# Two products instead of three for the last 32 gate channels of an RWKV output projection

## The chip, the cores and the metric

The kernel runs on one core of one Trainium2 chip. The metric is the device time of one execution in microseconds (us); the time before is 2402.96 us, the median of 3 runs (2399.5 to 2404.71). The verdict compares runs of the two kernels on the same chip.

## The reference, cut to what matters

A two-layer decoder trunk over 16 learned tokens and 512 tokens of 1024 channels. Layer 0 is an RWKV-7 time mixing between two half-step SwiGLU blocks, layer 1 a sparse attention between two more. Only the gate of the time mixing is touched here:

```python
D_GATE_LORA = 160
g = jax.nn.sigmoid(xg @ g1) @ g2              # g1: 1024 x 160, g2: 160 x 1024
...
return ((yn + bonus) * g) @ w_o               # the output projection, 1024 x 1024
```

## The kernel before, in words

Every product of the heavy matrices is done in three passes for precision. An operand is split into `hi`, its value in the shorter 32-bit type that the profile calls fp32r, and `lo`, what is left of it; `mm3` (L496) adds hi x hi, lo of the data x hi of the weights, and hi of the data x lo of the weights into one PSUM bank. The weights stream from DRAM in an order that is fixed ahead (`Weights`, L178): a unit is 1024 columns, SyncE loads it into `wraw`, ScalarE writes `whi`, VectorE writes `wlo` (L211), two units ahead of the product that takes them. So each unit costs ScalarE and VectorE one long instruction, and those stand in their queues between the others, in program order.

The tokens go through in two ranges, A (272 tokens, padded to 288) and B (256). For each range the time mixing has a projection stage (`proj`, L802; pools pA and pB), a chunked recurrence that is interleaved with other work by a planner (`run`, L729), and an output projection (`outproj`, L1270; pools oA and oB, L1352 and L1359). The planner orders side work by an estimated clock; what it decides after this change is the same order of instructions.

The gate stands in two places. In `proj`, step `g1` (L936 to L948), for each of 8 blocks of 128 input channels, two `mm3` go into two banks: 128 gate channels, then the last 32, with a stationary operand 32 columns wide. A sigmoid writes them to `R.sg`, the last 32 in partitions 0 to 31 of its second half. In `outproj`, `R.sg` is split into `shi` and `slo` (both named `lhi` and `llo` in the profile). Then `gate(m)` (L1279), for each of 8 blocks m of 128 output channels, does six products into a bank `bg`: three on 128 rows and three on 32 rows:

```python
for k, q in ((0, 128), (1, 32)):
    w = W.take(blk("g2", k, m))
    mm3(p[:, :n], (w[0][:q], w[1][:q]), (shi[:q, k, :n], slo[:q, k, :n]), k == 0, k == 1)
```

VectorE takes the bank, adds a bias to the recurrence's output and multiplies (`tb`), ScalarE writes `o_hi`, VectorE `o_lo`. These are the data of `wo`. The order is written by hand: gates 0 to 2; then for d = 0 to 7 the gate d + 3 (while there is one) and nine products of `wo` on `o[d]` into three banks; then the other five output blocks with 24 products each. On VectorE `tb` and `o_lo` of one gate stand one behind the other, so it waits for `o_hi` between them.

Of the kernel before, what the change touches and what calls it, by code (L numbers as in the profile page):

```python
# [10 lines left out]
F32 = mybir.dt.float32  # L11
F32R = mybir.dt.float32r
I32 = mybir.dt.int32
AF = mybir.ActivationFunctionType
OP = mybir.AluOpType
AX = mybir.AxisListType

D = 1024
DT = 8
# [32 lines left out]
def blk(key, k, m):  # L52
    return (key, k, m * 128, (m + 1) * 128)
# [124 lines left out]
class Weights:  # L178
# [32 lines left out]
    def split(self, last):  # L211

        while self.nlo <= min(last, len(self.units) - 1):
            self.round(self.nlo)
            r = self.raw.pop(self.nlo)
            w = r.shape[1]
            lo = self.pool.tile([128, 1024], F32R, name="wlo", bufs=self.bufs)
            self.nc.vector.tensor_sub(lo[:, :w], r, self.hi[self.nlo][:, :w].bitcast(F32))
            self.lo[self.nlo] = lo
            self.nlo += 1  # L220
# [213 lines left out]
def trunk(ctx, tc, wall, units, h0, vec, cstd, gqk, out, stop=None, gap=0.0, share=400.0, slack=200.0, fulls={}):  # L434
    clock = Clock()
    nc = Core(tc.nc, clock)
# [12 lines left out]
    W = Weights(nc, wpool, wall, units, raw_bufs=4, bufs=4, ahead=2)  # L449
# [46 lines left out]
    def mm3(p, w, x, first, last):  # L496

        nc.tensor.matmul(p, w[0], x[0], start=first, stop=False)
        nc.tensor.matmul(p, w[0], x[1], start=False, stop=False)
        nc.tensor.matmul(p, w[1], x[0], start=False, stop=last)  # L500

    def split(hi, lo, src, gp=False):
        nc.scalar.activation(hi, src, AF.Copy)
        if gp:
            nc.gpsimd.tensor_tensor(lo, src, hi.bitcast(F32), op=OP.subtract)
        else:
            nc.vector.tensor_sub(lo, src, hi.bitcast(F32))


    def newton(y, x, it, a):  # L510
# [291 lines left out]
    def proj(R, norm, sp, core, XB):  # L802

        r, n, pad, nch = R.r, R.n, R.pad, R.nch
# [14 lines left out]
        def mix(i, d):  # L819

            x = work.tile([128, 288], F32, name="tb", bufs=4)
            nc.vector.scalar_tensor_tensor(x[:, :n], xx[d // 4][:, d % 4, :n], col(MIX + 8 * i + d),
                                           hn[d][:, 1:1 + n], op0=OP.mult, op1=OP.add)
            hi = sp.tile([128, 288], F32R, name="xm_hi", bufs=XB)
            lo = sp.tile([128, 288], F32R, name="xm_lo", bufs=XB)

            def make():
                split(hi[:, :n], lo[:, :n], x[:, :n], gp=True)
                xm[i, d] = (hi[:, :n], lo[:, :n])

            if late:
                late.pop()()
            late.append(make)
# [70 lines left out]
        ps, pl, pg = {}, None, None  # L904
        for kind, *st in proj_steps():
            if kind == "d":
                key, g, ds = st
                if ds[0] == 0:
                    ps = [bank() for _ in range(4)]
                x = [need(mixof[key], d) for d in ds]  # L910
                mixes(len(ds))
                for m, p in enumerate(ps, 4 * g):
                    for d in ds:
                        w = W.take(blk(key, d, m))
                        yield p[:, :n], *w, *x[d - ds[0]]
                        mm3(p[:, :n], w, x[d - ds[0]], d == 0, d == DT - 1)
                    if ds[-1] == DT - 1:
                        evac(key, m, p[:, :n])
                free[0] += g * len(ds)
                mixes(g * len(ds))  # L920
                yield
            elif kind == "lora":
                key, d = st
                if pl is None:
                    pl = bbank("ry")
                mm3(pl[:, :n], W.take(blk(key, d, 0)), need(mixof[key], d), st == ["lw", 0], st == ["la", DT - 1])
                free[0] += 1
                mixes(1)
                if st == ["la", DT - 1]:
                    lora_end(pl)  # L930
                yield
            elif kind == "wa2":
                decay(st[0])
                yield
            elif kind in "EP":
                powers(kind, st[0])  # L936
            else:
                d = st[0]
                pg = pg or (bank(), bank())
                x = need(5, d)  # L940
                for m, k in ((0, 128), (1, 32)):
                    w = W.take(blk("g1", d, m))
                    mm3(pg[m][:k, :n], (w[0][:, :k], w[1][:, :k]), x, d == 0, d == DT - 1)
                free[0] += 1
                mixes(1)
                if d == DT - 1:
                    for i, k in ((0, 128), (1, 32)):
                        sg = R.sg[:k, i, :n]  # L948
                        nc.scalar.activation(sg, pg[i][:k, :n], AF.Sigmoid)
                yield  # L950
# [319 lines left out]
    def outproj(R, sp, nxt):  # L1270

        n, pad, r = R.n, R.pad, R.r
        shi = sp.tile([128, 2, 288], F32R, name="lhi")
        slo = sp.tile([128, 2, 288], F32R, name="llo")
        for i, k in ((0, 128), (1, 32)):
            split(shi[:k, i, :n], slo[:k, i, :n], R.sg[:k, i, :n])
        xs = {}

        def gate(m):  # L1279
            p = bbank()  # L1280
            for k, q in ((0, 128), (1, 32)):
                w = W.take(blk("g2", k, m))
                mm3(p[:, :n], (w[0][:q], w[1][:q]), (shi[:q, k, :n], slo[:q, k, :n]), k == 0, k == 1)
            t = work.tile([128, 288], F32, name="tb", bufs=4)
            nc.vector.scalar_tensor_tensor(chunks(t[:, :n]), R.AR[:, m, :R.nch, 1], col(LNB + m),
                                           chunks(p[:, :n]), op0=OP.add, op1=OP.mult)
            hi = sp.tile([128, 288], F32R, name="o_hi", bufs=8)
            lo = sp.tile([128, 288], F32R, name="o_lo", bufs=8)
            split(hi[:, :n], lo[:, :n], t[:, :n])
            xs[m] = (hi[:, :n], lo[:, :n])  # L1290

        def end(m, p):
            residual(m, r, p[:, pad:n], 1.0)
            nxt.add(m, r)

        for m in range(3):
            gate(m)
            yield
        ps = [bank() for _ in range(3)]
        for d in range(DT):  # L1300
            if d + 3 < DT:
                gate(d + 3)
            for m in range(3):
                mm3(ps[m][:, :n], W.take(blk("wo", d, m)), xs[d], d == 0, d == DT - 1)
            yield
        for m in range(3):
            end(m, ps[m])
        for m in range(3, DT):
            p = bank()
            for d in range(DT):  # L1310
                mm3(p[:, :n], W.take(blk("wo", d, m)), xs[d], d == 0, d == DT - 1)
                yield
            end(m, p)
# [404 lines left out]
def lay_out(i):  # L1718
    f = {k: np.asarray(v) for k, v in i.items()}

    def cols(a):
        return a.reshape(-1, DT, 128).transpose(2, 0, 1).reshape(128, -1)

    def qk_gain(a):

        return np.tile(np.concatenate([np.ones(16, np.float32), a[0, 16:]]), 2)[:, None]

    def pad(a, rows, width, c0=0):
        z = np.zeros((rows, width), np.float32)
        z[:a.shape[0], c0:c0 + a.shape[1]] = a  # L1730
        return z

    mats = {}
    for l in range(2):
        for j in range(2):
            mats[f"win{l}{j}"] = f["ffn_w_in"][l, j]
            mats[f"wout{l}{j}"] = f["ffn_w_out"][l, j]
    for k in "rkvo":
        mats["w" + k] = f["rk_w_" + k][0]
    mats["lw"] = pad(f["rk_w1"][0], D, 128)  # L1740
    mats["la"] = pad(f["rk_a1"][0], D, 128, 64)
    mats["wa2"] = np.concatenate([f["rk_w2"][0], f["rk_a2"][0]])
    mats["g1"] = pad(f["rk_g1"][0], D, 256)
    mats["g2"] = pad(f["rk_g2"][0], 256, D)
    w = f["at_w_in"][0]
    mats["idx"] = w[:, 1536:2120]
    mats["kvq"] = np.concatenate([w[:, 1024:1536], w[:, :1024]], 1)
    mats["ao"] = f["at_w_o"][0]
    vec = np.concatenate([cols(f["norm_g"]), cols(f["rk_mix"])] +
                         [cols(f["rk_" + k]) for k in ("w0", "a0", "k_k", "k_a", "r_k", "lnx_g", "lnx_b")] +  # L1750
                         [qk_gain(f["at_q_g"]), qk_gain(f["at_k_g"])], 1)
    h0 = np.concatenate([f["meta"], f["x"][0]], 0).T.reshape(DT, 128, T).transpose(1, 0, 2)
    return {"h0": np.ascontiguousarray(h0), "vec": np.ascontiguousarray(vec), "cst": constants(),
            "gqk": np.concatenate([f["at_q_g"], f["at_k_g"]], 0)}, mats
# [17 lines left out]
```

## Time and profile before

| | |
|---|---|
| median of 3 runs | 2402.96 us |
| the profiled execution's own time | 2405.28 us |
| its span, first to last instruction | 2403.5 us |
| TensorE (PE), matrix products | 2335.7 us busy, 97% |
| VectorE (DVE) | 1706.2 us, 71% |
| ScalarE (ACT) | 1263.9 us, 53% |
| GpSimd (POOL) | 169.5 us, 7% |
| mean granted TensorE clock | 0.982 of full speed |

The profile gives each instruction its start and duration. Products overlap in the profile: the time that one costs in a run of them is the distance of two starts, not the duration shown. The granted clock is shown as a share of 2.4 GHz: 1.00 is 2.4 GHz and 0.50 is 1.2 GHz, the two levels there are. The shape of a product is given as rows*columns of its stationary operand, then partitions x columns of the moving one: `32*128 32x256` is a product over 32 rows that gives 128 output channels for 256 tokens.

### The profile page before, as it was taken

To read this page: it belongs to the slowest core of one execution; us is meant where nothing else is said; L and a number is where in the kernel's file an instruction comes from. 1 tells how busy PE (TensorE), PEld (TensorE's weight loads), DVE (VectorE), ACT (ScalarE), POOL (GpSimd) and SP (SyncE) were. 2 spreads that over 40 slices of the span, in tenths; PEclk is the share of its full clock that TensorE was granted. 3 is DMA by queue.
4 is the path that set the end of the run, shared out by engine and by line. 5 is a ranking of instruction groups with operands and counts; after the bars stand their busy time and mean duration, and the time that the engine had idled before them with its cause. 6 is when DMAs were issued, how large, how long until landed. Compare 5 with 4: busy or idle time off the path is not lost.

```text
span 2403.5 us, 49406 instructions
## 1 busy us (share of the span) xinstructions
PE 2335.7 (97%) x20122; PEld 2189.8 (91%) x20122; DVE 1706.2 (71%) x3337; ACT 1263.9 (53%) x2125; POOL 169.5 (7%) x215
## 2 busy tenths in 40 slices
PE   8998999999889999999999999999999999999999
PEld 8997889998789899999999999799888888879999
DVE  7667888856787975576566566687767888666765
ACT  5443664456448535644444444456665546565543
POOL 0001521010043011000000000000000000000000
PEclk9999999999899999999999999999999999999999
DMA  6553335542334454244555555454434444425554
GB/s 228 174 177 114 125 125 172 172 133 72 106 115 159 153 164 133 81 132 153 176 176 167 186 190 177 140 168 142 150 122 138 141 144 133 139 78 168 177 185 141
DMA packets 101491, 356.13 MB, mean 148 GB/s; under 512 B 11520, under 2 KB 15632, under 8 KB 101264
## 3 DMA queue, kind: packets, MB, share of 16 engines
q1 hardware_dynamic: 99120, 347.91, 43.8%
q0 software_dynamic: 2144, 5.07, 0.8%
q8 instruction: 158, 2.59, 0.4%
q14 instruction: 69, 0.57, 0.1%
HBM read 348.60 MB, written 4.33 MB: 147 GB/s over the span
## 4 chain that ended last, share of the span: by engine, by line
PE 53%; DVE 2%; ACT 1%; issue 0%; DVEq 0%; ACTq 0%
PE acc L341 46%; PE bg L341 6%; PE ry L341 1%; DVE wlo L341 1%; DVE qst L341 0%; ACT whi L341 0%; DVE h L341 0%; DVE pr L341 0%; DVE tb L341 0%; DVE xa_lo L341 0%; DVE m L341 0%; DVE rel L341 0%; DVE nst L341 0%; DVE hid_lo L341 0%; ACT xa_hi L341 0%
## 5 line engine op out<-in xcount | busy, mean ns | idle before, releaser
L341 ACT ACTIVATE whi<-wraw 128x1024 fp32r<-128x1024 f32 (+1 forms) x658 | 688.5, 1051 | 465.2 <-PE acc L341 274.8
L341 DVE TENSOR_TENSOR wlo<-wraw,whi 128x1024 fp32r<-128x1024 f32 (+1 forms) x658 | 809.8, 1234 | 170.8 <-ACT whi L341 170.1
L341 PE MATMUL acc<-hid_hi,whi 128*128 128x256 f32 (+1 forms) x1408 | 412.1, 293 | 6.0 <-DVE h L341 5.9
L341 PE MATMUL acc<-hid_lo,whi 128*128 128x256 f32 (+1 forms) x1408 | 399.5, 284 | 0.0
L341 PE MATMUL acc<-hid_hi,wlo 128*128 128x256 f32 (+1 forms) x1408 | 399.4, 284 | 0.0
L341 PE MATMUL acc<-xa_hi,whi 128*128 128x256 f32 (+1 forms) x1088 | 316.4, 291 | 1.8 <-ACT xa_hi L341 1.4
L341 PE MATMUL acc<-x_hi,whi 128*128 128x272 f32 (+1 forms) x1024 | 303.1, 296 | 8.7 <-ACT whi L341 6.2
L341 PE MATMUL acc<-xa_hi,wlo 128*128 128x256 f32 (+1 forms) x1088 | 309.0, 284 | 0.1
L341 PE MATMUL acc<-xa_lo,whi 128*128 128x256 f32 (+1 forms) x1088 | 308.9, 284 | 0.1
L341 PE MATMUL acc<-x_hi,wlo 128*128 128x272 f32 (+1 forms) x1024 | 294.9, 288 | 0.5 <-DVE wlo L341 0.5
L341 PE MATMUL acc<-x_lo,whi 128*128 128x272 f32 (+1 forms) x1024 | 294.5, 288 | 0.1
L341 PEld LDWEIGHTS acc<-hid_hi,whi 128*128 128x128 f32 x1408 | 265.5, 189 | 23.0 <-issue 12.2
L341 PEld LDWEIGHTS acc<-hid_lo,whi 128*128 128x128 f32 x1408 | 266.9, 190 | 0.2 <-DVE hid_lo L341 0.2
L341 PEld LDWEIGHTS acc<-hid_hi,wlo 128*128 128x128 f32 x1408 | 265.8, 189 | 0.0
L341 PEld LDWEIGHTS acc<-xa_hi,whi 128*128 128x128 f32 x1088 | 206.2, 190 | 19.7 <-issue 17.1
L341 PE MATMUL acc<-xb_hi,whi 128*128 128x256 f32 x752 | 215.4, 286 | 0.0
L341 PE MATMUL acc<-xb_lo,whi 128*128 128x256 f32 x752 | 210.7, 280 | 0.0
L341 PE MATMUL acc<-xb_hi,wlo 128*128 128x256 f32 x752 | 210.6, 280 | 0.0
L341 PEld LDWEIGHTS acc<-x_hi,whi 128*128 128x128 f32 x1024 | 194.9, 190 | 15.2 <-ACT whi L341 6.2
L341 PEld LDWEIGHTS acc<-xa_lo,whi 128*128 128x128 f32 x1088 | 206.6, 190 | 0.6 <-DVE xa_lo L341 0.5
L341 PEld LDWEIGHTS acc<-xa_hi,wlo 128*128 128x128 f32 x1088 | 206.2, 190 | 0.4 <-DVE wlo L341 0.4
L341 PEld LDWEIGHTS acc<-x_hi,wlo 128*128 128x128 f32 x1024 | 194.7, 190 | 1.0 <-DVE wlo L341 1.0
(295 smaller groups left out, 4440.4 us busy)
## 6 DMA issues: line engine op xcount, KB each, us to landing
wraw<-wall SPq DMA_DIRECT2D x644, 512.0 KB, 3.3
wraw<-wall SPq DMA_DIRECT2D x10, 438.0 KB, 3.3
out<-h SPq DMA_DIRECT2D x8, 256.0 KB, 2.3
h<-h SPq DMA_DIRECT2D x2, 512.0 KB, 8.7
ynat<-L POOLq DMA_DIRECT2D x2, 512.0 KB, 4.4
T<-ynat POOLq DMA_DIRECT2D x2, 512.0 KB, 4.2
L<-gm POOLq DMA_DIRECT2D x14, 64.0 KB, 2.8
gm<-T POOLq DMA_DIRECT2D x4, 224.0 KB, 6.8
```

The source lines that it names most:

```text
L341: r = f(*args, **kw)
```

## The change

The weights are laid out so that the last 32 gate channels stand twice: columns 160 to 191 of `g1` repeat 128 to 159, and rows 160 to 191 of `g2` repeat rows 128 to 159; the rest up to 256 is zero, as before. So the second bank of `g1` is computed with a stationary operand of 128 columns, and the sigmoid writes 64 partitions, of which 32 to 63 are a copy of 0 to 31. In the output projection the second half of `shi` holds hi in partitions 0 to 31, lo in 32 to 63 and zeros in 64 to 127; the second half of `slo` holds hi in 0 to 31 and zeros elsewhere. One product of 128 rows of `shi` with the hi weights then gives hi x hi and lo x hi together, and one of `slo` with the lo weights gives hi x lo. GpSimd writes the zeros.

```diff
-                for m, k in ((0, 128), (1, 32)):
-                    w = W.take(blk("g1", d, m))
-                    mm3(pg[m][:k, :n], (w[0][:, :k], w[1][:, :k]), x, d == 0, d == DT - 1)
+                for m in range(2):
+                    mm3(pg[m][:, :n], W.take(blk("g1", d, m)), x, d == 0, d == DT - 1)
...
-                    for i, k in ((0, 128), (1, 32)):
+                    for i, k in ((0, 128), (1, 64)):
                         sg = R.sg[:k, i, :n]
...
-        for i, k in ((0, 128), (1, 32)):
-            split(shi[:k, i, :n], slo[:k, i, :n], R.sg[:k, i, :n])
+        nc.gpsimd.memset(shi[64:128, 1].bitcast(F32), 0.0)
+        nc.gpsimd.memset(slo[:, 1].bitcast(F32), 0.0)
+        split(shi[:, 0, :n], slo[:, 0, :n], R.sg[:, 0, :n])
+        nc.scalar.activation(shi[:64, 1, :n], R.sg[:64, 1, :n], AF.Copy)
+        nc.scalar.activation(slo[:32, 1, :n], R.sg[:32, 1, :n], AF.Copy)
+        e = shi[32:64, 1, :n]
+        nc.vector.tensor_sub(e, R.sg[32:64, 1, :n], e.bitcast(F32))
...
-            for k, q in ((0, 128), (1, 32)):
-                w = W.take(blk("g2", k, m))
-                mm3(p[:, :n], (w[0][:q], w[1][:q]), (shi[:q, k, :n], slo[:q, k, :n]), k == 0, k == 1)
+            mm3(p[:, :n], W.take(blk("g2", 0, m)), (shi[:, 0, :n], slo[:, 0, :n]), True, False)
+            w = W.take(blk("g2", 1, m))
+            nc.tensor.matmul(p[:, :n], w[0], shi[:, 1, :n], start=False, stop=False)
+            nc.tensor.matmul(p[:, :n], w[1], slo[:, 1, :n], start=False, stop=True)
...
+    a, b = f["rk_g1"][0], f["rk_g2"][0]
+    mats["g1"] = pad(np.concatenate([a, a[:, 128:]], 1), D, 256)
+    mats["g2"] = pad(np.concatenate([b, b[128:]], 0), 256, D)
```

(The `split` helper also loses an option for GpSimd, whose two instructions now stand where it was used; nothing comes of it.)

TensorE's queue at a gate of range B's output projection; `bg` rows are the gate's products, `acc` rows those of `wo`, and `-` rows are only before, `+` rows only after:

```order
 L341 MATMUL bg<-lhi,wlo 128x256
 L341 MATMUL bg<-lhi,whi 128x256
-L341 MATMUL bg<-llo,whi 128x256
-L341 MATMUL bg<-lhi,wlo 128x256
+L341 MATMUL bg<-llo,wlo 128x256
 L341 MATMUL acc<-o_hi,whi 128x256
 L341 MATMUL acc<-o_lo,whi 128x256
```

A gate has five products instead of six; each of the 16 gates (8 in each range) changes so, and no other row of TensorE's queue moves.

VectorE's queue from gate 3 to gate 6 of the same projection, in the kernel after the change; it reads the same before:

```order
1215 L341 TENSOR_TENSOR o_lo<-tb,o_hi 128x256
1216 L341 TENSOR_TENSOR wlo<-wraw,whi 128x1024
1217 L341 SCALAR_TENSOR_TENSOR tb<-AR,vecs,bg 128x256
1218 L341 TENSOR_TENSOR o_lo<-tb,o_hi 128x256
1219 L341 TENSOR_TENSOR wlo<-wraw,whi 128x1024
1220 L341 SCALAR_TENSOR_TENSOR tb<-AR,vecs,bg 128x256
1221 L341 TENSOR_TENSOR o_lo<-tb,o_hi 128x256
1222 L341 SCALAR_TENSOR_TENSOR tb<-AR,vecs,bg 128x256
1223 L341 TENSOR_TENSOR o_lo<-tb,o_hi 128x256
1224 L341 TENSOR_TENSOR wlo<-wraw,whi 128x1024
```

Nothing moved here: between the first `tb` and the last stand eight pairs and three splits of weights. Outside this stretch VectorE has the same number of instructions in the same order, ScalarE one copy more in each output projection, GpSimd two memsets more in each.

## Rows read from the trace of the kernel before

**Rows 1.** The page's first part: busy us, share of the span, instructions.

```profile
PE 2335.7 (97%) x20122; PEld 2189.8 (91%) x20122; DVE 1706.2 (71%) x3337; ACT 1263.9 (53%) x2125; POOL 169.5 (7%) x215
```

**Rows 2.** Timeline of PE, output projection A: start us, duration, instruction.

```profile
652.48 0.29 PE L341 MATMUL bg<-lhi,wlo 128*128 128x288 f32 x1
652.70 0.40 PE L341 MATMUL bg<-lhi,whi 32*128 32x288 f32 x1
652.94 0.29 PE L341 MATMUL bg<-llo,whi 32*128 32x288 f32 x1
653.07 0.29 PE L341 MATMUL bg<-lhi,wlo 32*128 32x288 f32 x1
653.29 0.40 PE L341 MATMUL acc<-o_hi,whi 128*128 128x288 f32 x1
```

**Rows 3.** The same view, output projection B, one gate.

```profile
1084.87 0.41 PE L341 MATMUL bg<-llo,whi 128*128 128x256 f32 x1
1085.08 0.41 PE L341 MATMUL bg<-lhi,wlo 128*128 128x256 f32 x1
1085.43 0.58 PE L341 MATMUL bg<-lhi,whi 32*128 32x256 f32 x1
1085.81 0.41 PE L341 MATMUL bg<-llo,whi 32*128 32x256 f32 x1
```

**Rows 4.** Stretches: length, busy PE, PEld, DVE, ACT, POOL, granted clock, DMA, GB/s.

```profile
1072.90:1089.50 16.60, 16.60 (x66) 14.38 (x65) 8.27 (x14) 5.28 (x9) 0.00 (x0) 0.50 0.25 87
1090.00:1110.00 20.00, 20.00 (x178) 19.97 (x178) 14.54 (x34) 10.28 (x16) 0.00 (x0) 1.00 0.44 150
1113.80:1117.00 3.20, 3.20 (x16) 3.20 (x15) 3.20 (x8) 1.11 (x3) 0.00 (x0) 0.50 0.22 46
1118.00:1127.00 9.00, 9.00 (x76) 9.00 (x75) 7.41 (x20) 5.05 (x7) 0.00 (x0) 1.00 0.43 138
```

**Rows 5.** The same view, output projection A.

```profile
632.90:646.00 13.10, 12.52 (x39) 9.61 (x39) 7.67 (x17) 3.94 (x7) 0.00 (x0) 0.50 0.16 47
646.20:658.00 11.80, 11.80 (x81) 10.82 (x81) 7.64 (x13) 4.63 (x7) 0.00 (x0) 1.00 0.40 130
```

**Rows 6.** Timeline of PE, last `wo` product of the first three banks, A and B.

```profile
658.04 0.29 PE L341 MATMUL acc<-o_hi,wlo 128*128 128x288 f32 x1
...
1094.26 0.28 PE L341 MATMUL acc<-o_hi,wlo 128*128 128x256 f32 x1
```

**Rows 7.** Timeline of DVE, projection B, gates 0 and 1.

```profile
1071.12 0.46 DVE L341 SCALAR_TENSOR_TENSOR tb<-AR,vecs,bg 128x256 f32<-128x256 f32 x1
...
1072.41 0.47 DVE L341 SCALAR_TENSOR_TENSOR tb<-AR,vecs,bg 128x256 f32<-128x256 f32 x1
```

**Rows 8.** The same view, projection A, start of gate 0.

```profile
634.33 1.21 DVE L341 TENSOR_TENSOR wlo<-wraw,whi 128x1024 fp32r<-128x1024 f32 x1
635.99 0.52 DVE L341 SCALAR_TENSOR_TENSOR tb<-AR,vecs,bg 128x288 f32<-128x288 f32 x1 [0.45 <-PE bg L341]
637.01 0.46 DVE L341 TENSOR_TENSOR o_lo<-tb,o_hi 128x288 fp32r<-128x288 f32 x1 [0.51 <-ACT o_hi L341]
```

**Rows 9.** Waits of DVE from 1069 to 1130 us: total, times, longest.

```profile
DVE tb L341 <- PE bg L341: 6.1, 4, 2.4
```

**Rows 10.** Timeline of PE, stage pB, step `g1`.

```profile
785.55 0.28 PE L341 MATMUL acc<-xm_hi,wlo 128*32 128x256 f32 x1
785.67 0.28 PE L341 MATMUL acc<-xm_hi,whi 128*128 128x256 f32 x1
785.79 0.28 PE L341 MATMUL acc<-xm_lo,whi 128*128 128x256 f32 x1
```

**Rows 11.** Timeline of ACT, projection B, first `o_hi`.

```profile
1071.62 0.42 ACT L341 ACTIVATE o_hi<-tb 128x256 fp32r<-128x256 f32 x1 [2.04 <-DVE tb L341]
```

**Rows 12.** Groups of POOL by form: count, busy us, mean ns, idle before.

```profile
L341 POOL MEMSET S<- 128x512 f32 x1 | 0.5, 544 | 0.0
```

**Rows 13.** Timeline of PE, second product of gate 0, projection B.

```profile
1069.79 0.38 PE L341 MATMUL bg<-llo,whi 128*128 128x256 f32 x1
```

More of the change, by code (lines that the diff above doesn't have):

```diff
@@ L500, in mm3, with split @@
         nc.tensor.matmul(p, w[1], x[0], start=False, stop=last)
-    def split(hi, lo, src, gp=False):
+    def split(hi, lo, src):
         nc.scalar.activation(hi, src, AF.Copy)
[L504 to L507, printed above, removed]
+        nc.vector.tensor_sub(lo, src, hi.bitcast(F32))
     def newton(y, x, it, a):
@@ L827, in make @@
             def make():
-                split(hi[:, :n], lo[:, :n], x[:, :n], gp=True)
+                nc.scalar.activation(hi[:, :n], x[:, :n], AF.Copy)
+                nc.gpsimd.tensor_tensor(lo[:, :n], x[:, :n], hi[:, :n].bitcast(F32), op=OP.subtract)
                 xm[i, d] = (hi[:, :n], lo[:, :n])
@@ L1742, in lay_out @@
     mats["wa2"] = np.concatenate([f["rk_w2"][0], f["rk_a2"][0]])
-    mats["g1"] = pad(f["rk_g1"][0], D, 256)
-    mats["g2"] = pad(f["rk_g2"][0], 256, D)
+    a, b = f["rk_g1"][0], f["rk_g2"][0]
+    mats["g1"] = pad(np.concatenate([a, a[:, 128:]], 1), D, 256)
+    mats["g2"] = pad(np.concatenate([b, b[128:]], 0), 256, D)
     w = f["at_w_in"][0]
```

## The prediction

> **What bounds the kernel now.** I read the page first: TensorE is busy for 97% of the span [rows 1], so time is won only where it works slowly or waits. Then the granted clock by stretches, which shows where it works slowly. From 1072.9 to 1089.5 us it is busy for all of 16.60 us, yet the clock is 0.50, that is 1.2 GHz; right behind, in 20 us just as full, it is 1.00 [rows 4]. The slow stretch is the gates of output projection B with the `wo` products between them. In projection A the clock is 0.50 from 632.9 to 646.0 and 1.00 behind it [rows 5]. Then the timeline of TensorE inside a gate, for the distance of two starts. Between two 32-row products it is 0.13 us (652.94 to 653.07). Going from 128 rows to 32 it is 0.22 and then 0.24, and going back 0.22 again [rows 2]. At the low clock the plain distance is 0.21, and going to 32 rows it is 0.35 and 0.38 [rows 3]. Last the waits of VectorE: from 1069 on it waits 6.1 us for the gates' banks [rows 9]. So TensorE sets the pace there and VectorE follows.
>
> **The change, part by part.**
>
> *The third small product.* Gone from 16 gates: 0.12 to 0.13 us each at the high clock, 0.21 to 0.24 at the low one. In B gates 3 to 7 lie in the low stretch, in A gates 0 to 4. 6 x 0.125 + 10 x 0.225 = 3.0 us of TensorE's time.
>
> *The change of row count.* All products of a gate now have 128 rows, as the `wo` products have. At the high clock the three late starts cost 0.09, 0.11 and 0.09 over 0.13 [rows 2]; I take the fourth like the second, so 0.40 us a gate. At the low clock one crossing costs 0.14 + 0.17 = 0.31 [rows 3], two of them 0.62. 6 x 0.40 + 10 x 0.62 = 8.6 us.
>
> The Trainium skill, TensorE: Matmul & The Clock Gate, section Why this matters for your kernels, says that a single matmul over 32 rows takes as long as one over 128, the gain lying in several at once. Among 32-row products the trace agrees (0.13); where the row count changes it does not. By that rule the full rows would be worth nothing and only the third product would go, 3.0 us.
>
> *The clock.* What distinguishes the slow stretch of B is not waiting: there is none in it. After a wait with 128-row products alone the clock was at 0.50 from 1113.8 to 1117.0 and back at 1.00 from 1118 [rows 4]; with gates between them it stayed low for 16.6 us. I read this as: products over few rows don't lift the clock. With full rows I expect B's clock to fall for no longer than those 3.2 us, or not at all, and A's, which fell in the waits before the gates, to rise some 3 to 6 us after 634 (once or twice that stretch, an estimate) instead of 12.
>
> *What is late next.* The terms above can't be added up, because VectorE takes over. Its order is unchanged: eight pairs `tb`, `o_lo`, and three splits of weights between the first `tb` and the last. From one `tb` to the next it takes 1.29 us where nothing else stands between (1071.12 to 1072.41) [rows 7]; a split is 1.21 [rows 8], some 1.15 of it in the queue, since neighbours overlap a little (an estimate from those rows). From a `tb`'s start to the end of its `o_lo` 1.02 + 0.46 pass in A [rows 8], some 1.4 in B.
> Projection B: first `tb` at 1071.1 as before (the split ahead of it sets it, not the gate); last `tb` 7 x 1.29 + 3 x 1.15 = 12.5 us later, 1083.6; its `o_lo` at 1085.0; nine `wo` products at 0.12 [rows 10], the last starting at 1086.0; before it started at 1094.26 [rows 6]. Gain 8.2 us. TensorE's own work is 40 gate and 72 `wo` products, 112 x 0.12 = 13.4 us from 1069.8 [rows 13], done at 1083.2; so it waits some 3 us for VectorE.
> Projection A: first `tb` at 635.5, when the split that starts at 634.33 ends, instead of 635.99 after a wait of 0.45 for gate 0 [rows 8]. Pitch 1.37 (0.08 more than in B, for 288 columns). Last `tb` 9.6 + 3.45 later, 648.6; its `o_lo` at 650.1; the last product starts at 651.2. TensorE's side: gate 0 begins at 632.9 with 0.58 us idle [rows 5], so 112 x 0.13 = 14.6 us from 634.1 is 648.7, plus half of the 3 to 6 us at the low clock: 650 to 652. I take 652.0, the later end, since both sides meet there, against 658.04 before [rows 6]. Gain 6.0 us.
> Of the sum, 14.2, I keep 1.6 us back for one more fall of the clock in TensorE's new waits: 3.2 us at half speed, as in [rows 4]. That leaves 12.6 us.
>
> *The step `g1`.* 48 products in each range get a stationary operand of 128 columns instead of 32. The distance of starts is 0.12 behind the narrow one and 0.12 behind the wide one [rows 10]: nothing. The sigmoid does 64 partitions instead of 32 in the same columns: nothing. No bytes are added, the blocks were 128 wide before.
>
> *The added preparation.* One ScalarE copy for each range, 0.42 us like [rows 11], stands between the copies of `shi` and the first `o_hi`; ScalarE idles 2.04 us there [rows 11], so it costs nothing; without that cover, 0.4 us per range. Two memsets of up to 288 columns on GpSimd, under 0.54 us each by one of 512 columns [rows 12]; GpSimd is not busy at all in these stretches [rows 4, 5]. Both must wait until the store that `shi` and `slo` take over is read out, as the first `shi` copy does. If they were late, the fifth product of gate 0 would be, by at most 1.1 us per range; the split of weights on VectorE would hide most of it. Behind the memsets on GpSimd nothing is due until the next stage.
>
> Behind both projections the order on every engine is the same as before, so what is won there stays won; VectorE is busy for 14.54 of 20 us behind B [rows 4] and can follow. The profiled execution took 2405.28 us, 2.3 above the median of the runs. 2405.28 - 12.6 = 2392.7; put on the median, 2402.96 - 12.6 = 2390.4.
>
> **The rivals.**
>
> 1. *The clock stays as it was.* It might not depend on the rows. Say it is low until the same moments, 646.0 and 1089.5. A: 50 of 112 products done by 646.0 at 0.24 (0.21 of [rows 3] for 288 columns instead of 256), the other 62 take 8.1 us, done at 654.1, gain 3.9. B: 26 done by 1072.9, 79 more at 0.21 until 1089.5, the last 7 by 1090.3, gain 4.0. Sum 7.9 us, 2395.1. For it: A's fall was due to waits, which stay. Against it: the full but slow 16.6 us of B, which no wait explains.
> The Trainium skill, TensorE: Matmul & The Clock Gate, Part 1 (The HAM clock gate), says that the clock follows how busy the engine has been of late, and names no rows; by that the change would leave the clock alone and this rival's time would come. [Rows 4] speak against the rule as it stands: busy for 16.60 of 16.60 us at 0.50.
>
> 2. *Only the third product goes.* The late starts at a change of rows would come back in another form (for instance because they are loads of weights that wait for a bank), or VectorE's pace is worse than 1.29 and eats the rest: 2403.0 - 3.0 = 2400.0. Against it: 0.13 between equal row counts, hi and lo weights alike [rows 2].
>
> 3. *Slower: TensorE starves and the clock stays down.* With VectorE as the pace, TensorE waits some 3 us in B, in pieces before each `wo` group. If these waits kept the clock at 0.50 through the rest of the projections, the 20 us behind B's gates [rows 4] would become 40; less the 4.0 of rival 1, B alone would lose 16, and the time would be some 2419 or more. It decides from the point where the low clock lasts some 25 us longer than now in the two together, since each of these costs half and 12.6 are won. Against it: at the low clock a gate with its nine products takes 14 x 0.21 = 2.9 us, longer than VectorE's 1.3 to 2.4 (with or without a split), so TensorE no longer waits and the full-row products lift the clock, as from 1118 on [rows 4].
>
> 4. *More than forecast.* `o_hi` and `o_lo` come sooner than VectorE's pitch says, and TensorE's own work sets both ends: 1083.2 and 648.7, 11.1 + 9.3 = 20.4 us, 2382.6.
>
> **How the numbers follow.** Forecast 0.65, rival 1 0.17, rival 2 0.10, rival 3 0.03, rival 4 0.05. The time is the forecast's, 2390.5. The range goes down to rival 4's 2383, and up past rival 1 (2395.1) to 2398, where the preparation's 0.4 and 1.1 us per range, uncovered, would put it; it leaves out rivals 2 and 3. Some 0.2% (4.8 us) is what a measurement of this kernel can tell from no change: the forecast, rival 1 and rival 4 lie beyond it, 0.87; rival 2 lies within, 0.10; rival 3 is slower, 0.03.
>
> **What would show it.** The profile after should show, in a gate, five starts 0.12 to 0.13 apart at the high clock; a granted clock near 1.00 in B's gates but for a few us, and in A from about 640; new waits of PE `acc` for DVE `o_lo`, with the wait of `tb` for PE `bg` nearly gone; the last of the first `wo` products some 16 us after gate 0 of B began, where it was 24.5. The sum is wrong if `tb` follows `tb` by much more than 1.3 us, if the clock is still at 0.50 for over 10 us in B, or if starts in a gate stay 0.2 apart. It is wrong elsewhere if time comes or goes outside the two projections by more than 2 us.

## The result, and the profile after

| | before | after |
|---|---|---|
| median of the runs of one job | 2401.23 us (4 runs, 2398.1 to 2404.71) | 2388.22 us (4 runs, 2385.19 to 2389.66) |
| profiled execution | 2405.28 us, span 2403.5 | 2388.85 us, span 2387.1 |
| mean granted clock | 0.982 | 0.986 |

The ratio after to before is 0.9948, 95% interval 0.9932 to 0.9965: faster, by 13.0 us between the medians (forecast 12.6, 2390.5 us). A second comparison on another chip, with five rounds, gave 0.9941 (0.9918 to 0.9964). The two profiled executions lie further apart, 16.4 us, since that of before was a late one (2405.28, above all four runs of the table). Where the trace is used below, it is this 16.4 that is taken apart.

The page's first part, to be held against [rows 1]: TensorE has 16 products less, the third small one of 16 gates, and is busy 17.4 us less. Its share stays at 97%.

```profile
PE 2318.3 (97%) x20106; PEld 2178.6 (91%) x20106; DVE 1703.6 (71%) x3337; ACT 1264.4 (53%) x2127; POOL 171.5 (7%) x219
```

The stretches of after, columns as in [rows 4]: two of projection A, the gates and first `wo` products of projection B, and the work that stood at 1113.8 to 1117.0 in [rows 4], which runs some 15 us earlier now.

```profile
631.90:638.30 6.40, 5.36 (x20) 5.00 (x21) 5.32 (x16) 2.74 (x7) 0.00 (x0) 0.50 0.24 83
638.40:651.00 12.60, 12.50 (x93) 12.29 (x93) 9.04 (x16) 6.34 (x11) 0.00 (x0) 0.99 0.38 124
1060.00:1078.80 18.80, 15.92 (x117) 14.06 (x116) 13.34 (x25) 8.94 (x18) 0.67 (x2) 1.00 0.34 109
1098.80:1102.00 3.20, 3.20 (x29) 3.20 (x27) 3.20 (x8) 1.09 (x3) 0.00 (x0) 1.00 0.25 42
```

The slow stretch of B is gone: 16.6 us at 0.50 before [rows 4], 1.00 from 1060 to 1078.8 now. In A the clock still falls in the waits ahead of the gates, but is back at 638.3 instead of 646 [rows 5].

One trace is one execution. A second trace of the changed kernel (after5, below) does have a short fall of the clock in the gates of B, and one in the work that stood at 1113.8 before. Its stretches, then its second product of gate 0 and its last `wo` product of the first three banks in B:

```profile
1064.30:1067.50 3.20, 3.20 (x15) 3.20 (x16) 2.24 (x4) 0.85 (x3) 0.00 (x0) 0.50 0.33 101
1098.50:1101.70 3.20, 3.20 (x13) 3.01 (x14) 3.20 (x8) 1.54 (x4) 0.81 (x3) 0.50 0.66 205
```

```profile
1063.68 0.39 PE L341 MATMUL bg<-llo,whi 128*128 128x256 f32 x1
...
1080.12 0.28 PE L341 MATMUL acc<-o_hi,wlo 128*128 128x256 f32 x1
```

So with full rows the clock can still fall in B, for some 3 us and not for 16.6. This fall costs nothing there: the stretch takes 1080.12 - 1063.68 = 16.44 us, and in after, without a fall, 16.43 (below).

The timeline of TensorE in after: second product of gate 0 and last `wo` product of the first three banks in A; then in B the second to fourth product of gate 0, a whole gate, the two new waits, and the last `wo` product of the first three banks.

```profile
633.55 0.61 PE L341 MATMUL bg<-llo,whi 128*128 128x288 f32 x1 [0.58 <-DVE llo L341]
...
650.88 0.29 PE L341 MATMUL acc<-o_hi,wlo 128*128 128x288 f32 x1
...
1062.28 0.39 PE L341 MATMUL bg<-llo,whi 128*128 128x256 f32 x1
1062.50 0.28 PE L341 MATMUL bg<-lhi,wlo 128*128 128x256 f32 x1
1062.82 0.36 PE L341 MATMUL bg<-lhi,whi 128*128 128x256 f32 x1
...
1066.33 0.28 PE L341 MATMUL bg<-lhi,whi 128*128 128x256 f32 x1
1066.45 0.28 PE L341 MATMUL bg<-llo,whi 128*128 128x256 f32 x1
1066.57 0.28 PE L341 MATMUL bg<-lhi,wlo 128*128 128x256 f32 x1
1066.69 0.28 PE L341 MATMUL bg<-lhi,whi 128*128 128x256 f32 x1
1066.80 0.28 PE L341 MATMUL bg<-llo,wlo 128*128 128x256 f32 x1
1066.92 0.28 PE L341 MATMUL acc<-o_hi,whi 128*128 128x256 f32 x1
...
1073.60 0.39 PE L341 MATMUL acc<-o_hi,whi 128*128 128x256 f32 x1 [0.56 <-ACT o_hi L341]
...
1077.34 0.39 PE L341 MATMUL acc<-o_hi,whi 128*128 128x256 f32 x1 [0.77 <-ACT o_hi L341]
...
1078.71 0.28 PE L341 MATMUL acc<-o_hi,wlo 128*128 128x256 f32 x1
```

Five starts of a gate now follow each other at 0.12 us, and so does the first `wo` product behind them; the late starts of [rows 2, 3] are gone there. From the second product of gate 0 in B to the last `wo` product of the first three banks it is 1078.71 - 1062.28 = 16.43 us; before it was 1094.26 - 1069.79 = 24.47 [rows 6, 13]. That is **8.0 us** won in B. In A it is 650.88 - 633.55 = 17.33. Before, the second product of gate 0 in A stood here in the same view:

```profile
634.09 0.61 PE L341 MATMUL bg<-llo,whi 128*128 128x288 f32 x1 [0.58 <-DVE llo L341]
```

658.04 [rows 6] - 634.09 = 23.95. That is **6.6 us** won in A. Together 14.7 of the 16.4; the remaining 1.8 us lie in other stages.

The trace of before is that of a late execution. The run g1only (below) has the same gates, and its profiled execution (2399.77 us) lies nearer to the median of before: there A takes 656.67 - 632.73 = 23.94 us, and B, from the first of these products to the second, 22.96:

```profile
1068.45 0.39 PE L341 MATMUL bg<-llo,whi 128*128 128x256 f32 x1
...
1091.41 0.28 PE L341 MATMUL acc<-o_hi,wlo 128*128 128x256 f32 x1
```

Against these the changed kernel wins 6.6 and 6.5 us, 13.1 in all, which is nearly what lies between the medians.

VectorE in after, in B, from the first `tb` to the last:

```profile
1063.85 0.47 DVE L341 SCALAR_TENSOR_TENSOR tb<-AR,vecs,bg 128x256 f32<-128x256 f32 x1
1064.81 0.42 DVE L341 TENSOR_TENSOR o_lo<-tb,o_hi 128x256 fp32r<-128x256 f32 x1 [0.48 <-ACT o_hi L341]
1065.15 0.47 DVE L341 SCALAR_TENSOR_TENSOR tb<-AR,vecs,bg 128x256 f32<-128x256 f32 x1
...
1076.36 0.47 DVE L341 SCALAR_TENSOR_TENSOR tb<-AR,vecs,bg 128x256 f32<-128x256 f32 x1
```

The waits of the gates in B (1060 to 1079), of TensorE first, then of VectorE: total, times, longest.

```profile
PE acc L341 <- ACT o_hi L341: 1.3, 2, 0.8
PE bg L341 <- ACT lhi L341: 1.3, 1, 1.3
...
DVE o_lo L341 <- ACT o_hi L341: 3.9, 8, 0.5
```

VectorE no longer waits for the banks of the gates, 6.1 us before [rows 9]. From the first `tb` to the last it runs without a gap but for the 0.48 us inside each gate in which ScalarE makes `o_hi`. TensorE is now the one that waits in the gates, 1.3 us in two pieces; the 1.3 us ahead of gate 0 (the line with `lhi`) stood there before too.

### The profile page after: what moved, and what is told of

Read it like the earlier page. It is cut to its first block, busy times and chain, and to the rows that moved or that the text cites. A ratio compares the mean times of both kernels' runs of the same rounds, so it can differ in the third digit from the quotient of the medians.

```text
span 2387.1 us, 49385 instructions
## 1 busy us (share of the span) xinstructions
PE 2318.3 (97%) x20106; PEld 2178.6 (91%) x20106; DVE 1703.6 (71%) x3337; ACT 1264.4 (53%) x2127; POOL 171.5 (7%) x219
## 4 chain that ended last, share of the span: by engine, by line
PE 85%; DVE 9%; ACT 3%; issue 1%; DMA 1%; POOL 0%; SPq 0%; DVEq 0%; ACTq 0%; POOLq 0%
PE acc L341 72%; PE bg L341 10%; PE ry L341 4%; DVE wlo L341 3%; DVE tb L341 1%; ACT whi L341 1%; DMA wraw<-wall 1%; DVE st L341 1%; DVE ynat L341 1%; ACT bu L341 1%; DVE bu L341 1%; DVE h L341 0%; DVE nst L341 0%; DVE ss L341 0%; DVE AR L341 0%
## 5 line engine op out<-in xcount | busy, mean ns | idle before, releaser
L341 PEld LDWEIGHTS acc<-xa_hi,whi 128*128 128x128 f32 x1088 | 206.5, 190 | 20.3 <-issue 17.1
```

The source lines that it names most:

```text
L341: r = f(*args, **kw)
```

## The experiments

The theory: 32-row products next to full-row ones cost TensorE late starts and hold the clock down; full rows end both; behind that VectorE's order sets the pace. The rivals: it was the third product alone; it was something else in the change (the wider step `g1`, the preparation); or the clock alone, or the late starts alone. Runs named together in one job share the runs of the kernel before. Diffs are against the changed kernel where nothing else is said.

**full3: full rows, but three products.** The small half of the gate is zero-padded to 128 rows and keeps its three products, six in a gate as before.

```diff
-        nc.gpsimd.memset(shi[64:128, 1].bitcast(F32), 0.0)
+        nc.gpsimd.memset(shi[:, 1].bitcast(F32), 0.0)
...
+        for i, k in ((0, 128), (1, 32)):
+            split(shi[:k, i, :n], slo[:k, i, :n], R.sg[:k, i, :n])
...
-            mm3(p[:, :n], W.take(blk("g2", 0, m)), (shi[:, 0, :n], slo[:, 0, :n]), True, False)
-            w = W.take(blk("g2", 1, m))
-            nc.tensor.matmul(p[:, :n], w[0], shi[:, 1, :n], start=False, stop=False)
-            nc.tensor.matmul(p[:, :n], w[1], slo[:, 1, :n], start=False, stop=True)
+            for k in range(2):
+                mm3(p[:, :n], W.take(blk("g2", k, m)), (shi[:, k, :n], slo[:, k, :n]), k == 0, k == 1)
```

> Full rows, but three products for the last 32 channels again (hi and lo separately, padded with zero rows); six products a gate, all over 128 rows. Theory R (the change of row count and the low clock cost the time): 16 products more, 2 us of TensorE's time, most of it under VectorE's pace; 0 to 2 us over the changed kernel, 2388 to 2391 us, clock 1.00 in the gates of projection B, starts 0.12 to 0.13 us apart. Theory N (the gain is that of the third product): back at the kernel before, about 2401 us.

Measured: 2390.14 us (2387.07 to 2391.71), ratio to before 0.9949 (0.9936 to 0.9963). The gain is there with all six products. So it is the rows and not the number of products. Second product of gate 0 and last `wo` product of the first three banks in B:

```profile
1062.86 0.39 PE L341 MATMUL bg<-llo,whi 128*128 128x256 f32 x1
...
1079.09 0.28 PE L341 MATMUL acc<-o_hi,wlo 128*128 128x256 f32 x1
```

That is 16.23 us, and in A it is 652.66 - 635.26 = 17.40; after has 16.43 and 17.33. So the third product costs nothing in these stretches of the trace, and the 2 us between this median and that of after, from different jobs, are not resolved.

**rows64: two products, but over 64 and 32 rows.** The same instructions as the changed kernel, cut to the rows that hold data.

```diff
-            nc.tensor.matmul(p[:, :n], w[0], shi[:, 1, :n], start=False, stop=False)
-            nc.tensor.matmul(p[:, :n], w[1], slo[:, 1, :n], start=False, stop=True)
+            nc.tensor.matmul(p[:, :n], w[0][:64], shi[:64, 1, :n], start=False, stop=False)
+            nc.tensor.matmul(p[:, :n], w[1][:32], slo[:32, 1, :n], start=False, stop=True)
```

> Two products as in the change, but over 64 rows (hi and lo) and 32 rows (hi), not padded to 128. R: three crossings of row count a gate (128 to 64, 64 to 32, 32 to 128) at 0.2 us or, at the low clock, 0.3 us each; clock 0.50 through the gates of B as before; only the third product's 2 to 4 us of the gain remain or less, 2397 to 2401 us. N: all of the gain remains, about 2388 us.

Measured: 2402.49 us (10 runs), ratio 1.0012 (0.9997 to 1.0028): none of the gain, and 1.5 us over the expected range. One gate of its timeline in B:

```profile
1083.06 0.41 PE L341 MATMUL bg<-lhi,wlo 128*128 128x256 f32 x1
1083.41 0.58 PE L341 MATMUL bg<-lhi,whi 64*128 64x256 f32 x1
1083.92 0.58 PE L341 MATMUL bg<-llo,wlo 32*128 32x256 f32 x1
1084.42 0.58 PE L341 MATMUL acc<-o_hi,whi 128*128 128x256 f32 x1
```

and the stretch:

```profile
1079.00:1096.00 17.00, 17.00 (x61) 13.68 (x60) 8.18 (x14) 4.97 (x9) 0.00 (x0) 0.50 0.22 77
```

Three changes of row count (128 to 64, 64 to 32, 32 to 128) make distances of 0.35, 0.51 and 0.50 us where 0.21 is plain at this clock: 0.73 us late in these three alone, more than the 0.62 for the two changes of the kernel before. The clock is at 0.50 for 17 busy microseconds, as before the change.

**rows96: two products over 96 rows.** 

```diff
-            nc.tensor.matmul(p[:, :n], w[0], shi[:, 1, :n], start=False, stop=False)
-            nc.tensor.matmul(p[:, :n], w[1], slo[:, 1, :n], start=False, stop=True)
+            nc.tensor.matmul(p[:, :n], w[0][:96], shi[:96, 1, :n], start=False, stop=False)
+            nc.tensor.matmul(p[:, :n], w[1][:96], slo[:96, 1, :n], start=False, stop=True)
```

> The changed kernel with its two padded products over 96 rows instead of 128. If every change of row count costs, two crossings a gate come back and the time lies near that of rows64, 2395 to 2400 us; if a product over 96 rows follows one over 128 like another over 128, and holds the clock, the time is that of the changed kernel, 2388 us.

Measured, one run: 2388.68 us beside 2400.68 for before in the same job, which is the changed kernel's time. A gate in B:

```profile
1066.71 0.28 PE L341 MATMUL bg<-lhi,wlo 128*128 128x256 f32 x1
1066.83 0.28 PE L341 MATMUL bg<-lhi,whi 96*128 96x256 f32 x1
1066.95 0.28 PE L341 MATMUL bg<-llo,wlo 96*128 96x256 f32 x1
1067.07 0.28 PE L341 MATMUL acc<-o_hi,whi 128*128 128x256 f32 x1
```

So not every change of row count starts late: from 128 to 96 and back the distance stays 0.12. With 64 and 32 rows it does not.

**g1only: the wider step `g1` alone**, with the gate and its preparation as before. Against the kernel before:

```diff
-                for m, k in ((0, 128), (1, 32)):
-                    w = W.take(blk("g1", d, m))
-                    mm3(pg[m][:k, :n], (w[0][:, :k], w[1][:, :k]), x, d == 0, d == DT - 1)
+                for m in range(2):
+                    mm3(pg[m][:, :n], W.take(blk("g1", d, m)), x, d == 0, d == DT - 1)
...
-                    for i, k in ((0, 128), (1, 32)):
+                    for i, k in ((0, 128), (1, 64)):
```

> Only the wider step g1 of the change (stationary operand of 128 columns, sigmoid of 64 partitions); the gates as before, six products with 32 rows. Forecast of its own term: nothing, within 2 us of the kernel before (about 2401). If the wider load cost or the fuller array helped the clock there, it would differ by over 3 us.

Measured: 2400.11 us (10 runs), ratio 1.0003 (0.9988 to 1.0018). The wider weights and sigmoid are worth nothing that these runs resolve (the interval reaches from 3 us faster to 4 us slower).

**cross: the kernel before, its six products alternating 128 and 32 rows.** Same products, six changes of row count in a gate instead of two.

```diff
-            for k, q in ((0, 128), (1, 32)):
-                w = W.take(blk("g2", k, m))
-                mm3(p[:, :n], (w[0][:q], w[1][:q]), (shi[:q, k, :n], slo[:q, k, :n]), k == 0, k == 1)
+            w, v = W.take(blk("g2", 0, m)), W.take(blk("g2", 1, m))
+            for j, (a, b) in enumerate(((0, 0), (0, 1), (1, 0))):
+                x = (shi, slo)[b]
+                nc.tensor.matmul(p[:, :n], w[a], x[:, 0, :n], start=j == 0, stop=False)
+                nc.tensor.matmul(p[:, :n], v[a][:32], x[:32, 1, :n], start=False, stop=j == 2)
```

> The kernel before with the same six products a gate in alternating order: 128, 32, 128, 32, 128, 32 rows, so six crossings of row count for two. R: four crossings more in each of 16 gates at 0.2 us (high clock) to 0.3 us (low): 13 to 20 us slower than before, 2414 to 2421 us, and every start in a gate 0.2 us or more behind the last. N (the number of products counts): no change, 2401 us.

Measured, one run: 2422.27 us beside 2400.68, 21.6 us more, above the range that was expected. A gate and the `wo` product behind it in B (x2 is a pair of 128 and 32 rows, shown as one row):

```profile
1094.01 0.92 PE L341 MATMUL bg<-lhi,whi 128*128 128x256 f32 x2
1094.87 1.09 PE L341 MATMUL bg<-llo,whi 128*128 128x256 f32 x2
1095.88 1.09 PE L341 MATMUL bg<-lhi,wlo 128*128 128x256 f32 x2
1096.90 0.58 PE L341 MATMUL acc<-o_hi,whi 128*128 128x256 f32 x1
```

The last two pairs take 1.01 and 1.02 us, 0.51 for each start instead of 0.21: each change of row count costs 0.30 us at the low clock. The prediction's 0.31 came from two late starts in [rows 3]. The clock stays low longer as well: in B the stretch 1090 to 1106 has 0.50, and 1.00 stands only from 1111 on, some 30 us after the fall at 1079 (16.6 us before the change, [rows 4]). That is the likely reason why the time lies over the expected range.

**few4 and full4: the small half four times over, with 32 and with 128 rows.** A run of twelve products over few rows has no change of row count inside it, so late starts and few rows come apart; in both kernels the last 32 channels count four times in the result. few4 is against the kernel before, full4 is full3 with the same loop over all 128 rows:

```diff
-            for k, q in ((0, 128), (1, 32)):
-                w = W.take(blk("g2", k, m))
-                mm3(p[:, :n], (w[0][:q], w[1][:q]), (shi[:q, k, :n], slo[:q, k, :n]), k == 0, k == 1)
+            mm3(p[:, :n], W.take(blk("g2", 0, m)), (shi[:, 0, :n], slo[:, 0, :n]), True, False)
+            w = W.take(blk("g2", 1, m))
+            for j in range(4):
+                mm3(p[:, :n], (w[0][:32], w[1][:32]), (shi[:32, 1, :n], slo[:32, 1, :n]), False, j == 3)
```

> The kernel before with the three 32-row products of each gate done four times over (so the last 32 channels count four times): 12 in a row over 32 rows, still two crossings. Tells apart why the clock is low. If products over few rows keep it low: 0.50 from gate 0 or 1 to the end of the gates in both projections, and 144 products more at 0.21 to 0.24 us, about 2433 us. If the late starts at the crossings keep it low: they are a smaller part now, so the clock rises within some us, and the products cost 0.12 to 0.13, about 2415 us.

> The kernel full3 with its three padded products done four times over (the last 32 channels count four times): as many products as few4, all over 128 rows. R: clock 1.00 in the gates of B, 0.50 in A only for some us after the waits; 144 products more than full3 at 0.12 to 0.13 us, 18 us, less the 3 us in which TensorE waited for VectorE: 2402 to 2407 us. If dense gates lower the clock whatever the rows, it is as slow as few4.

Measured, one run each in one job: few4 2423.36 us, full4 2401.04 us (1 us under its range). Both have 20266 products on TensorE; the 22.3 us between them are due to the rows, with the late starts that few4 has at the ends of its runs. Stretches of few4 in B: the first three gates with gate 3, the nine `wo` products behind them, and what follows; then the whole of full4's gates there.

```profile
1083.80:1097.50 13.70, 13.70 (x58) 12.13 (x56) 3.23 (x7) 2.19 (x4) 0.00 (x0) 0.50 0.12 39
1097.50:1100.40 2.90, 2.90 (x14) 2.68 (x13) 2.04 (x3) 1.37 (x2) 0.00 (x0) 0.50 0.00 0
1101.00:1111.00 10.00, 10.00 (x79) 9.21 (x78) 4.99 (x8) 2.20 (x4) 0.00 (x0) 1.00 0.30 105
```

```profile
1069.00:1091.00 22.00, 20.62 (x176) 20.21 (x175) 13.42 (x25) 7.92 (x16) 0.61 (x2) 1.00 0.27 86
```

In the 13.7 us, four of five products have 32 rows, most of them at the plain distance:

```profile
1090.83 0.58 PE L341 MATMUL bg<-lhi,whi 32*128 32x256 f32 x1
1091.21 0.41 PE L341 MATMUL bg<-llo,whi 32*128 32x256 f32 x1
1091.43 0.41 PE L341 MATMUL bg<-lhi,wlo 32*128 32x256 f32 x1
```

They lie 0.21 apart, TensorE has no gap, and the clock stays at 0.50. It rises some 3 us after nine `wo` products over full rows began. So this dense run of few-row products did not lift the clock; that the late starts at its two ends, a few among fifteen products, are not what kept it low is likely, but not shown. And few4's expectation was too strong: the time lay between its two figures, because from 1101 on the clock stays at 1.00 although each gate still has its twelve 32-row products. In few4 the clock rose behind the first run of twelve full-row products (nine of `wo`, three of the next gate, 1097.5 to 1100.3). The kernel before has such runs too, from 1075.0 on, and its clock rose only behind the fourth of them. So few rows do not explain by themselves how long the clock stayed low before; the late starts, closer together there, may have a part in it.

**pipe and pipe5: VectorE's order changed.** In the changed kernel, VectorE makes `o_lo` of a gate only after `tb` of the next one, so that it does not stand still while ScalarE makes `o_hi`.

```diff
-        xs = {}
+        xs, late = {}, []
+
+        def rest():
+            if late:
+                late.pop()()
...
-            split(hi[:, :n], lo[:, :n], t[:, :n])
+            nc.scalar.activation(hi[:, :n], t[:, :n], AF.Copy)
+            rest()
+            late.append(lambda: nc.vector.tensor_sub(lo[:, :n], t[:, :n], hi[:, :n].bitcast(F32)))
```

(`rest` is also called behind the last gate.)

> The changed kernel with o_lo of one gate put behind tb of the next on VectorE, so that VectorE does not wait for o_hi between them. If VectorE's pitch of 1.3 us sets the end of projection B, as the forecast says, TensorE's own 13.4 us take its place there (16.4 in the changed kernel): 3 us won in B, up to 0.5 in A, about 2385 us. If something else paces it (ScalarE's o_hi, the banks, the weights), no gain: 2388 us.

Measured: 2384.32 us (5 runs), ratio to before 0.9927 (0.9914 to 0.9939). Since the changed kernel had been timed on another chip, both were timed again beside each other, with the reordering alone in the kernel before (pipe_old) as a third:

> The changed kernel once more, as the yardstick for the two versions beside it, whose earlier times come from another chip. The ratio to the kernel before should lie in the interval that its first comparison gave, 0.993 to 0.9965.

> The changed kernel with o_lo of a gate behind tb of the next on VectorE, measured beside the changed kernel. If VectorE's pace holds the changed kernel's gates up (its two new waits in B are 1.3 us together, its one in A 0.4), this one is faster by 2 to 5 us. If what it gained earlier was only the difference of two chips, the two times agree within 1.5 us.

> The same reordering in the kernel before, with its six products and 32 rows. Theory: before the change TensorE set the pace in the gates (VectorE waited 6.1 us for their banks) and VectorE became the pace only through the change; then the reordering alone is worth nothing here, ratio to the kernel before 0.999 to 1.001 (within 2.4 us). Rival: VectorE's order cost time before the change too; then it gains the same 2 to 5 us as in the changed kernel.

| five rounds, one job | median us | ratio to before (2399.1) |
|---|---|---|
| the changed kernel (after5) | 2388.16 (2386.38 to 2390.19) | 0.9941 (0.9918 to 0.9964) |
| with VectorE reordered (pipe5) | 2383.04 (2381.08 to 2385.62) | 0.9923 (0.9897 to 0.9948) |
| before, VectorE reordered (pipe_old) | 2398.57 (2396.92 to 2405.42) | 0.999 (0.9974 to 1.0006) |

pipe5 is 5.1 us under the changed kernel, and the two sets of six runs do not touch. VectorE and TensorE of pipe5 in B:

```profile
1064.06 0.47 DVE L341 SCALAR_TENSOR_TENSOR tb<-AR,vecs,bg 128x256 f32<-128x256 f32 x1
...
1064.79 0.47 DVE L341 SCALAR_TENSOR_TENSOR tb<-AR,vecs,bg 128x256 f32<-128x256 f32 x1
```

```profile
1061.19 0.38 PE L341 MATMUL bg<-llo,whi 128*128 128x256 f32 x1
...
1074.76 0.28 PE L341 MATMUL acc<-o_hi,wlo 128*128 128x256 f32 x1
```

`tb` now follows `tb` after 0.73 us instead of 1.30, and the stretch in B takes 1074.76 - 1061.19 = 13.57 us instead of 16.44 in after5, near TensorE's own 13.4 (112 products at 0.12). TensorE has no wait there but the one ahead of gate 0. In A it is 16.21 us (633.70 to 649.91) instead of 17.33. The two stretches make 4.0 of the 5.1 us; where the rest comes from was not traced.

In pipe_old the same edit gives 0.5 us between the medians. Its interval reaches down to 0.9974, some 6 us, and so would not shut out pipe5's gain by itself. The trace speaks more clearly: the stretch in B takes 22.95 us (1075.96 to 1098.91), and 22.96 in g1only, whose VectorE has the old order. There VectorE has to wait for TensorE's banks whatever its own order (waits from 1074 to 1100: total, times, longest):

```profile
DVE tb L341 <- PE bg L341: 8.7, 7, 3.0
```

pipe5 is the fastest version found, and it beats both kernels.

## Why the prediction was right, point by point

- **The third product (3.0 us).** The prediction said that it could not simply be added, because VectorE takes over. It is hidden entirely: full3 keeps it, and its last `wo` product comes 16.23 us after the second product of gate 0 in B, as early as after's.
- **The change of row count (0.40 us a gate at the high clock, 0.62 at the low).** At the high clock the starts that were late in [rows 2, 3] are 0.12 apart. cross measured 0.30 for one change at the low clock, for 0.31.
- **The clock.** "Products over few rows don't lift the clock" was read off [rows 4] and agrees with few4's 13.7 us at 0.50 against full4's 22 us at 1.00, with the same number of products; as a rule it is too strong, as few4 shows from 1101 on. A's rise, expected between 3 and 6 us after 634, came at 638.3. B's clock did not fall in after and fell for some 3 us in after5; the prediction allowed both.
- **Late starts and clock, each alone.** How much each gave can only be estimated from the rows. In A the clock is low for 4.8 us behind the second product of gate 0 (633.55 to 638.3) instead of 11.9 (634.09 to 646.0); half of the difference is 3.6 us, and 6.6 were won. In B eight gates at 0.62 make 5.0 us of late starts at most, and 8.0 were won. So the clock alone does not make A's gain, nor the late starts alone B's.
- **VectorE takes over.** First to last `tb` in B: 12.5 us forecast, 1076.36 - 1063.85 = 12.51 measured; last `wo` product 16.2 us after the second product of gate 0 forecast, 16.43 measured. TensorE loses 16.43 - 13.4 = 3.0 us, as forecast (some 3), of which 1.3 are the two new waits and the rest starts that are late by less. The waits were foreseen for `o_lo` and ahead of every group; the profile shows two and puts them down to `o_hi`, which also waits for VectorE's `tb`. pipe5 and pipe_old show from two sides that VectorE's order became the bound through the change.
- **A.** Forecast 6.0, measured 6.6. The prediction took TensorE's later end, 652.0, which is 17.9 us after the second product at 634.1; VectorE's side gave 651.2, 17.1 us after it. Measured are 17.33, so VectorE sets the end in A too: last `tb` 14.5 us after that product forecast (648.6), 648.31 - 633.55 = 14.8 measured. In after5 the clock is low for less long behind that product (634.46 to 637.6), and the stretch takes 17.33 us again; with VectorE reordered (pipe5) it takes 16.21.
- **The 1.6 us kept back** for one more fall of the clock were wrong by their mechanism. In after TensorE waited in B, 0.56 and 0.77 us, and the clock stayed at 1.00; in after5 it did fall, for some 3 us, and the stretch took 16.44 us all the same. With VectorE setting the end, that fall cost nothing.
- **Luck in the sum.** Without that term the forecast was 14.2 us, and the two profiled executions show 14.7. But the forecast was read from a late execution of the kernel before, in which B took 24.47 us; with g1only's 22.96 the same reading gives 1.5 us less. The wrong 1.6 us made up for that, and so 12.6 lies close to the 13.0 between the medians. The interval of the ratio holds anything from 8 to 16 us and does not judge either term; the traces do.
- **`g1` and the preparation.** g1only shows nothing. In the preparation the memsets on GpSimd end only just in time (1060.63 to 1061.36 in B; gate 0 begins at 1061.82, behind a wait of 1.30 us for ScalarE's copies that stood there before), and the operations of the small half come a little late: the fourth product of gate 0 in B starts 0.32 behind the third instead of 0.12. ScalarE idles still 1.97 us before the first `o_hi` in B (2.04 in [rows 11]), so the added copy is covered.
- **Rival 1** (the clock stays) is out: 1.00 throughout B in after, 0.50 for some 3 us in after5. The Trainium skill, TensorE: Matmul & The Clock Gate, Part 1 (The HAM clock gate), lets the clock follow how busy the engine was and names no rows. few4 speaks against it as it stands: TensorE is busy for 13.70 of 13.70 us at 0.50.
- **Rival 2** (only the third product) is out by full3, which keeps that product and has the gain, and by rows64, which drops it and has none. The Trainium skill, TensorE: Matmul & The Clock Gate, section Why this matters for your kernels, gives a single product over 32 rows the time of one over 128; few4 agrees inside its runs (0.21 for both) and the changes of row count do not.
- **Rival 3** (starved and slow): TensorE waited as feared, and the clock fell for some 3 us in one of the two traces of the changed kernel and not in the other; it did not stay down.
- **Rival 4** (TensorE's own end, 20.4 us won) did not come with this change, as VectorE stood in the way. With VectorE reordered B's stretch took 13.57 us, for 13.4; A's took 16.21, for 14.6, as the low clock at its start stays (0.50 from 630.5 to 637.0 in pipe5). pipe5 is 16.1 us under the kernel before.
- **Elsewhere**, 1.8 us came (16.43 between the profiled executions less 14.66), within the 2 us allowed. Some of it are falls of the clock in other stages that one execution has and another has not: the fall at 1113.8 of [rows 4] is missing at its place in after, and after5 has it (1098.5), so the change did not remove it. It isn't settled what moves those.

## What to carry to other kernels

Where TensorE is fully busy and the granted clock is 0.50, look for products over few rows among full ones: padding them to full rows with zeros can be faster than leaving rows out, as full3 shows, even with no product saved. After such a gain look at once at who sets the pace now: here a reordering on VectorE that showed no gain before the change gave 5.1 us after it. And look at more than one trace of the same kernel: two of the changed kernel differ in where the clock falls, and only the second shows that a fall need not cost anything while another engine sets the end.

## What was not expected of the hardware

- 96 rows behave like 128 beside full rows (starts 0.12 apart, the changed kernel's time), 64 and 32 rows do not (in rows64 up to 0.31 from start to start at the high clock and 0.51 at the low). Why the boundary lies between 64 and 96, and whether it does for other column counts, was not tried.
- Once the clock is up, gates with twelve 32-row products among fifteen, with nine full-row products between them, left it up (few4, 1101 to 1111: 1.00). In the kernel before, gates with three such products stood in 16.6 us at 0.50. What decides between the two, and how the late starts play into it, stays open: no run had late starts with full rows alone.
- Two waits of 0.56 and 0.77 us in full-row work left the clock at 1.00 in after. In after5, the same kernel, the clock was at 0.50 from 1064.3 to 1067.5, and the projection ended no later for it.
